# Stores of the latent queries' pairs of heads, written as one store of 64 rows for each head

## The chip, the cores and the metric

The kernel runs on one core of one Trainium2 chip. The metric is the device time of one execution in microseconds (us), as the median of several runs. A measurement of this kernel can tell about 0.2% (5.5 us) from no change. The core has TensorE (PE in the profile), VectorE (DVE), ScalarE (ACT), GpSimd (POOL) and SyncE (SP). All DMAs of this kernel are issued by SP, in one order, on one queue, and the bytes are moved by the core's 16 DMA engines.

## The reference, cut to what matters

Two layers run over 512 latent tokens and 256 context tokens. In each layer, one input projection feeds three attention branches. The change touches the first of them, multi-head latent attention (MLA), and of that only the queries: a normed latent of 384 features is projected to 8 heads of 96 features, 64 plain ones and 32 rotated ones.

```python
def mla_heads(qc, kvc, kr, q_norm, w_uq, kv_norm, w_ukv, rope):
    b, n = qc.shape[:2]
    q = (rms_norm(qc, q_norm) @ w_uq).reshape(b, n, MLA_HEADS, MLA_NOPE + MLA_ROPE)
    ...
    q_nope, q_rot = q[..., :MLA_NOPE], q[..., MLA_NOPE:]
    ...
    return (jnp.concatenate([q_nope, q_rot], axis=-1), jnp.concatenate([k_nope, k_rot], axis=-1), v)
```

## The kernel before, in words

All tensors are float32. Every matrix product is done as three products of rounded parts: a value x is split into a high part H, rounded by ACT, and a low part L = x - H, made by DVE. A weight item goes the same way: SP loads it into a tile `ws` (two buffers), ACT makes `wh` high and DVE makes `wh` low, and only then can PE use it. A `ws` buffer is loaded again when both parts of its last item are made.

The order of the work is written by a planner (`Plan`), which runs while the program is built. It keeps an estimated time for each engine and for the DMA queue (`dma_t`: 620 ns for each issue on the queue, then the bytes at 350 bytes per ns for all engines together), and it interleaves two streams of work. One stream is attention (scores into tiles `wd`, softmax, transposes by the helper at L913, products into `bk`); the other is the list `SEQ` of projections with their weights. What the planner writes is a fixed order for each engine.

The projections of the MLA queries stand near the head of each layer's list, as `cr p0 p1 Q3 p2 p3`, beside the attention of the windowed branch. `cr` makes the rotated features of all heads and stores them with four DMAs of 8 heads x 16 rows. Each `p` makes the plain features of a pair of heads: PE writes 128 rows (two heads of 64) and up to 768 tokens into `bk`, ACT and DVE make H and L in two slots (tiles `s`, from a pool of 46), and both are stored to the DRAM tensors `q_d`, of 8 heads x 96 rows x 768 tokens. The attention reads them back much later, head by head (the first of these loads is issued at 788.1 us). A slot is free for its next user when its store has landed; the function `chain` inside `uq_h` (L1368) tells the planner the estimated time of that. In layer 0 a stored row is 768 tokens (3072 bytes, 384 KB for a pair), in layer 1 it is 512 tokens (2048 bytes, 256 KB).

SP issues DMAs strictly in order. The DMAs signal their landing on eight semaphores in turn, so that a DMA also waits for the one issued eight before it.

Of the kernel before, what the change touches and what calls it, by code (L numbers as in the profile page):

```python
# [16 lines left out]
F32 = mybir.dt.float32  # L17
# [8 lines left out]
CT, LT, T = 256, 512, 768  # L26
# [209 lines left out]
def hybrid_kernel(tc, x_in, c_in, ctx_in, c_ctx, w_mod, b_mod, norm_g, w_in, q_norm, w_uq, kv_norm, w_ukv,  # L236
# [20 lines left out]
    def slot(dt=F32, cols=T):  # L257
        Slots.left -= 1
        assert Slots.left >= 0
        return sb.tile([128, cols], dt, name=nm("s"), tag="slot", bufs=NS)  # L260

    def free(n, when=None):
        def later():
            yield when
            Slots.left += n
        if when is None:
            Slots.left += n
        else:
            P.spawn(later(), 0)
# [77 lines left out]
    def dmas(ready, pairs):  # L347
        yield ready
        t = 0.0
        for o, i in pairs:  # L350
            t = max(t, dma(o, i))
        return t
# [21 lines left out]
    q_d = [[dr.tile([8, 96, T], F32, name=f"q{l}{s}") for s in range(2)] for l in range(2)]  # L374
# [4 lines left out]
    def wl_in(w, c0, k0=0, kn=8, n=128):  # L379
        def load(t):  # L380
            return [(t[:, 0:kn * n].rearrange("p (k c) -> p k c", k=kn),
                     w[k0 * 128:(k0 + kn) * 128, c0:c0 + n].rearrange("(k p) c -> p k c", p=128))]
        return load

    def item(load, parts=None, split=True, size=1024):

        done = When()
        return dict(load=load, parts=parts, split=split, size=size, ready=When(), done=done, staged=When() if split else done)
# [50 lines left out]
    def v3(it, k, n, off=0):  # L439
        return [it[s][:, off:off + k * n].rearrange("p (k c) -> p k c", k=k) for s in ("H", "L")]  # L440
# [21 lines left out]
    def fm(it, wv, X, kn, lat=True, ctx=True):  # L462

        r = {}
        if lat:
            r["l"] = {}
            yield from fm_part(it, wv, X, kn, CT, LT, bk.gate, r["l"])
        if ctx:
            r["c"] = {}
            yield from fm_part(it, wv, X, kn, 0, CT, bk.gate, r["c"])  # L470
        return r

    def split_to(t, src, H, L, scale=1.0, psum=True):

        t1 = yield from act(t, H, src, scale=scale, psum=psum)
        if scale == 1.0:
            t2 = yield from tt(t1, L, src, H.bitcast(F32), ALU.subtract)
        else:
            t2 = yield from stt(t1, L, src, scale, H.bitcast(F32), ALU.mult, ALU.subtract)
        return t2  # L480
# [717 lines left out]
    def entry(handler, its=(), need=0, keep=0, gate=0.0, ahead=False):  # L1198
        part[0].append((handler, list(its), need, keep, gate, ahead))
# [86 lines left out]
    def build_layer(o):  # L1286
        l = o.l
# [7 lines left out]
        def sec_q():  # L1295
# [18 lines left out]
            c0q = 0 if cx else CT  # L1314
# [44 lines left out]
            for pr in range(4):  # L1359
                pv = (lambda t: t[:, 0:384].rearrange("p (k h c) -> p k h c", k=3, h=2),  # L1360
                      lambda t: t[:, 0:576].rearrange("p (k h c) -> p k h c", k=3, h=2)[:, :, :, 0:64])
                n_it = item(wl_in(w_uq[l], pr * 192, kn=3, n=192), parts=[pv])

                def uq_h(it, pr=pr):
                    H, L = slot(F32R), slot(F32R)
                    r = yield from fm(it, v3(it, 3, 128), o.cq, 3, ctx=cx)

                    def chain():  # L1368
                        t = 0.0
                        for key, a, n in (("l", CT, LT), ("c", 0, CT)):  # L1370
                            if key in r:
                                t = yield from split_to(r[key]["t"], r[key]["ps"][:, 0:n], H[:, a:a + n], L[:, a:a + n])
                                r[key]["rel"].t = t
                        prs = []
                        for i, S_ in enumerate((H, L)):
                            prs.append((q_d[l][i][2 * pr:2 * pr + 2, 0:64, c0q:T], S_[:, c0q:T].bitcast(F32)))
                        t = yield from dmas(t, prs)
                        free(2, t)
                        yield o.qrt
                        for hh in range(2):  # L1380
                            o.qd[2 * pr + hh].t = max(t, o.qrt.t)
                    P.spawn(chain())
                    o.uses["cq"] -= 1
                    if not o.uses["cq"]:
                        free(6, P.now)
                entry(uq_h, [n_it], need=2)
# [537 lines left out]
```

## Time and profile before

| | |
|---|---|
| median of 3 runs | 2775.6 us (2774.97 to 2778.2) |
| the profiled execution, its own time | 2790.33 us |
| its span in the trace | 2788.6 us |
| PE busy | 2678.3 us, 96% of the span |
| DVE busy | 1656.1 us, 59% |
| ACT busy | 1382.4 us, 50% |
| mean DMA rate | 89 GB/s |
| pair stores in the program | 16 (4 pairs x H and L x 2 layers) |

PE is the engine with the most work, so its busy share is the first thing to read, then the stretches in which it is idle, and what ended them. In a table by windows, each engine has its busy time in the window with the number of its instructions in parentheses (in the order PE, PEld, DVE, ACT, POOL). The last three columns are the granted TensorE clock (1.00 is 2.4 GHz, 0.50 is 1.2 GHz), the mean busy share of the 16 DMA engines, and GB/s.

### The profile page before, as it was taken

Reading aid. Unit: us, or ns where it says so; the run is one execution under the profiler, and the core shown is the slowest. Engines: PE = TensorE matmul, PEld = TensorE weight load, DVE = VectorE, ACT = ScalarE, POOL = GpSimd, SP = SyncE. Lnnn points to the kernel's source line nnn. Section 1 sums busy time; section 2 is a strip of 40 time slices with the busy share of each in tenths; the row PEclk is TensorE's granted clock in tenths of the full one; section 3 lists DMA queues with packets and bytes.
Section 4 is the critical chain, followed back from the end, with each engine's and each line's share of the span. In section 5 each row is a group of like instructions: output and inputs, shape, how many; then the busy total and the mean of one; then the engine's idle time right before and its main releaser. Section 6 shows DMA issues by size and latency. Waiting matters only on the chain.

```text
span 2788.6 us, 42903 instructions
## 1 busy us (share of the span) xinstructions
PE 2678.3 (96%) x16711; PEld 2325.5 (83%) x16711; DVE 1656.1 (59%) x3350; ACT 1382.4 (50%) x2860; POOL 129.7 (5%) x198
## 2 busy tenths in 40 slices
PE   7998999999999999999999998899999999999998
PEld 4887898888888878878888987788888889888888
DVE  4676778666676652132423567698767677634435
ACT  4666777555556541121222356687645555523322
POOL 0000000111100000000000000000101100000000
PEclk8989999999999999999999999999999999999999
DMA  6123221111123353343322532322111123444433
GB/s 230 44 67 99 59 55 47 48 42 53 43 69 88 105 182 106 113 156 91 95 80 61 170 104 62 97 66 59 48 47 52 50 74 92 128 120 125 122 102 129
DMA packets 327867, 249.57 MB, mean 89 GB/s; under 512 B 24068, under 2 KB 287840, under 8 KB 327664
## 3 DMA queue, kind: packets, MB, share of 16 engines
q1 hardware_dynamic: 327664, 246.83, 30.2%
q8 instruction: 131, 2.15, 0.3%
q14 instruction: 72, 0.59, 0.1%
HBM read 211.37 MB, written 35.41 MB: 88 GB/s over the span
## 4 chain that ended last, share of the span: by engine, by line
PE 76%; DVE 8%; ACT 6%; DMA 5%; issue 3%; POOL 1%; SPq 1%; DVEq 0%; ACTq 0%; POOLq 0%
PE wd L444 36%; PE bk L444 34%; PE bk L913 4%; ACT s L309 3%; ACT pt L309 3%; DMA ws<-in_w_in_dram 2%; DVE pt L323 2%; DVE s L323 1%; DMA q<-s 1%; DVE wh L323 1%; DVE s L858 1%; PE bk L579 1%; DMA s<-in_w_mod_dram 1%; DVE s L330 1%; ACT wh L309 1%
## 5 line engine op out<-in xcount | busy, mean ns | idle before, releaser
L444 PE MATMUL wd<-s,wh 128*128 128x512 f32 (+1 forms) x4392 | 857.0, 356 | 7.0 <-ACT wh L309 3.8
L444 PEld LDWEIGHTS wd<-s,wh 128*128 128x128 f32 x4392 | 726.7, 190 | 145.8 <-ACT s L309 12.9
L444 PE MATMUL bk<-s,wh 128*128 128x512 f32 (+1 forms) x3666 | 778.6, 358 | 17.8 <-DVE s L323 6.8
L444 PEld LDWEIGHTS bk<-s,wh 128*128 128x128 f32 x3666 | 587.6, 191 | 107.3 <-DVE s L323 10.0
L323 DVE TENSOR_TENSOR wh<-ws,wh 128x1024 fp32r<-128x1024 f32 (+4 forms) x294 | 325.3, 1112 | 352.9 <-ACT wh L309 349.5
L309 ACT ACTIVATE wh<-ws 128x1024 fp32r<-128x1024 f32 (+4 forms) x294 | 282.8, 968 | 316.2 <-PE wd L444 148.7
L309 ACT ACTIVATE pt<-bk 128x512 fp32r<-128x512 f32 (+3 forms) x604 | 341.6, 584 | 171.6 <-PE bk L913 103.5
L444 PE MATMUL bk<-wh,s 128*128 128x256 f32 x2688 | 354.9, 287 | 3.8 <-DVE wh L323 2.0
L444 PEld LDWEIGHTS bk<-wh,s 128*128 128x128 f32 x2688 | 335.4, 194 | 9.5 <-issue 3.2
L323 DVE TENSOR_TENSOR pt<-bk,pt 128x512 fp32r<-128x512 f32 (+3 forms) x400 | 257.9, 664 | 87.9 <-ACT pt L309 77.1
L444 PE MATMUL bk<-pt,s 128*128 128x256 f32 x1888 | 282.3, 291 | 25.5 <-DVE pt L323 20.1
L444 PEld LDWEIGHTS bk<-pt,s 128*128 128x128 f32 x1888 | 256.3, 194 | 52.3 <-DVE pt L323 27.3
L444 PE MATMUL wd<-s,s 128*128 128x256 f32 (+5 forms) x1872 | 277.4, 334 | 12.2 <-DVE ti L858 6.6
L309 ACT ACTIVATE s<-wd,ti 128x768 f32<-128x768 f32 (+1 forms) x240 | 195.5, 818 | 140.8 <-DVE ti L825 78.6
L444 PEld LDWEIGHTS wd<-s,s 64*128 64x128 f32 (+2 forms) x1872 | 215.6, 191 | 43.0 <-ACT s L309 9.9
L913 PE MATMUL bk<-ident,s 128*128 128x128 f32 x1472 | 211.1, 278 | 15.8 <-DVE s L323 5.5
L913 PEld LDWEIGHTS bk<-ident,s 128*128 128x128 f32 x1472 | 172.1, 143 | 42.2 <-ACT s L309 7.6
L309 ACT ACTIVATE s<-s,ti 128x512 f32<-128x512 f32 (+3 forms) x249 | 174.4, 709 | 14.3 <-DVE ti L865 7.0
L309 ACT ACTIVATE s<-bk 128x256 fp32r<-128x256 f32 (+5 forms) x291 | 113.7, 424 | 92.6 <-PE bk L444 85.5
L330 DVE SCALAR_TENSOR_TENSOR s<-s,wd 128x768 f32<-128x768 f32 (+1 forms) x58 | 47.6, 820 | 180.7 <-PE wd L444 108.3
L309 ACT ACTIVATE s<-wd 128x768 f32<-128x768 f32 (+1 forms) x58 | 40.9, 705 | 219.3 <-PE wd L444 219.1
L825 DVE TENSOR_REDUCE ti<-wd 128x1 f32<-128x768 f32 (+1 forms) x160 | 128.8, 844 | 18.6 <-PE wd L444 18.3
(98 smaller groups left out, 1742.7 us busy)
## 6 DMA issues: line engine op xcount, KB each, us to landing
ws<-in_w_in_dram SPq DMA_DIRECT2D x180, 512.0 KB
ws<-in_w_branch_dram SPq DMA_DIRECT2D x48, 512.0 KB
ws<-in_w_mod_dram SPq DMA_DIRECT2D x32, 512.0 KB
ws<-in_w_out_dram SPq DMA_DIRECT2D x24, 512.0 KB
y<-yo SPq DMA_DIRECT2D x80, 128.0 KB
s<-y SPq DMA_DIRECT2D x24, 384.0 KB
s<-s SPq DMA_DIRECT2D x22, 384.0 KB
s<-in_w_mod_dram SPq DMA_DIRECT2D x32, 256.0 KB
```

What stands on the lines that cost most here:

```text
L309: lambda: nc.scalar.activation(out=out, in_=in_, func=func, scale=scale, **kw))
L323: t = yield from dve(ready, lambda: nc.vector.tensor_tensor(out=out, in0=a, in1=b, op=op), n)
L330: t = yield from dve(ready, lambda: nc.vector.scalar_tensor_tensor(out=out, in0=a, scalar=s, in1=b, op0=op0, op1=op1), fsz(out), ptr=ptr)
L444: nc.tensor.matmul(o, lhsT=l, rhs=r, start=first, stop=last)
L579: nc.tensor.matmul(pm[32 * g:32 * g + 32, :], lhsT=sil[:, kt], rhs=wv, start=kt < 4, stop=kt >= 4)
L825: t = yield from dve(t, lambda: nc.vector.tensor_reduce(out=nmx, in_=p[:, lo:hi], axis=AX.X, op=ALU.max, negate=True), n)
L858: t = yield from dve(t, lambda: nc.vector.tensor_tensor_reduce(out=pt_[:, 0:n], in0=p[:, lo:hi], in1=mk, scale=1.0, scalar=sk, op0=ALU.add ...
L913: nc.tensor.transpose(out=pp[:, j * 256 + ri2 * 128:j * 256 + ri2 * 128 + 128], in_=row["P"][:, c:c + 128], identity=ident)
```

## The change

The tuple of slices that `dmas` stores is built for each head of the pair instead of for the pair. Before, the DRAM side is a block of 2 heads x 64 rows x tokens, filled from the 128 rows of one slot. Now there are two stores of 64 rows x tokens each. The bytes, their rows and their places in DRAM are the same; the pair stores become 32 instead of 16.

```diff
                         for i, S_ in enumerate((H, L)):
-                            prs.append((q_d[l][i][2 * pr:2 * pr + 2, 0:64, c0q:T], S_[:, c0q:T].bitcast(F32)))
+                            for hh in range(2):
+                                prs.append((q_d[l][i][2 * pr + hh, 0:64, c0q:T], S_[hh * 64:hh * 64 + 64, c0q:T].bitcast(F32)))
```

On the SP queue of layer 1, where the first two pairs and the rotated features are stored, this stood before (`q` are the stores to `q_d`, `ws` weight loads, `y` stores of attention outputs from `yo`; the last numbers are the shape of what is written):

```order
L341 DMA y_99<-yo_17438 64x128 x2
L341 DMA q_104<-s_17514 2x64x512
L341 DMA q_105<-s_17515 2x64x512
L341 DMA q_104<-s_17447 8x16x512
L341 DMA q_104<-s_17449 8x16x512
L341 DMA q_105<-s_17448 8x16x512
L341 DMA q_105<-s_17450 8x16x512
L341 DMA q_104<-s_17559 2x64x512
L341 DMA q_105<-s_17560 2x64x512
L341 DMA ws_17648<-in_mla_w_uq_dram 128x3x192
L341 DMA ws_17684<-in_w_in_dram 128x8x128
```

The same place on the SP queue after the change:

```order
L341 DMA y_99<-yo_17446 64x128 x2
L341 DMA q_104<-s_17522 64x512 x2
L341 DMA q_105<-s_17523 64x512 x2
L341 DMA q_104<-s_17455 8x16x512
L341 DMA q_104<-s_17457 8x16x512
L341 DMA q_105<-s_17456 8x16x512
L341 DMA q_105<-s_17458 8x16x512
L341 DMA q_104<-s_17567 64x512 x2
L341 DMA q_105<-s_17568 64x512 x2
L341 DMA ws_17654<-in_mla_w_uq_dram 128x3x192
L341 DMA ws_17696<-in_w_in_dram 128x8x128
```

Nothing has moved against anything else here: each pair store has become two in its place, and the weight load behind them has four more DMAs ahead of it. At the other seven places of the queue it is the same.

The planner's estimates move with the number of DMAs, and in one place of the whole program another order came out of them. It is on PE, a few matmuls after the first pair stores of layer 1. Before, between two rows of scores (tiles `wd`), one round of transposes stood alone:

```order
L913 MATMUL bk_66<-ident,s_17474 128x128
L913 MATMUL bk_66<-ident,s_17486 128x128
L444 MATMUL wd_71<-s_16532,s_16906 128x384
L444 MATMUL wd_71<-s_16533,s_16906 128x384
L444 MATMUL wd_71<-s_16532,s_16906 128x256
L444 MATMUL wd_71<-s_16533,s_16906 128x256
L913 MATMUL bk_67<-ident,s_17474 128x128
L913 MATMUL bk_67<-ident,s_17486 128x128
L444 MATMUL wd_70<-s_16532,s_16907 128x384
L444 MATMUL wd_70<-s_16533,s_16907 128x384
```

After the change, the same place on PE:

```order
L913 MATMUL bk_66<-ident,s_17482 128x128
L913 MATMUL bk_66<-ident,s_17494 128x128
L913 MATMUL bk_67<-ident,s_17482 128x128
L913 MATMUL bk_67<-ident,s_17494 128x128
L444 MATMUL wd_71<-s_16540,s_16914 128x384
L444 MATMUL wd_71<-s_16541,s_16914 128x384
L444 MATMUL wd_71<-s_16540,s_16914 128x256
L444 MATMUL wd_71<-s_16541,s_16914 128x256
L444 MATMUL wd_70<-s_16540,s_16915 128x384
L444 MATMUL wd_70<-s_16541,s_16915 128x384
```

Two transposes moved ahead of four score matmuls. The orders of DVE, ACT and POOL are the same in both programs.

## Rows read from the trace of the kernel before

**Rows 1.** The page: busy time of the engines; the last chain by line.
```profile
PE 2678.3 (96%) x16711; PEld 2325.5 (83%) x16711; DVE 1656.1 (59%) x3350; ACT 1382.4 (50%) x2860; POOL 129.7 (5%) x198
PE wd L444 36%; PE bk L444 34%; PE bk L913 4%; ACT s L309 3%; ACT pt L309 3%; DMA ws<-in_w_in_dram 2%; DVE pt L323 2%; DVE s L323 1%; DMA q<-s 1%; DVE wh L323 1%; DVE s L858 1%; PE bk L579 1%; DMA s<-in_w_mod_dram 1%; DVE s L330 1%; ACT wh L309 1%
```

**Rows 2.** Chain that ended last, 200:262 and 1715:1800: start us, us, what.
```profile
214.72 18.07 DMA q<-s
235.28 18.41 DMA ws<-in_w_in_dram
...
1722.85 13.30 DMA q<-s
1738.00 14.81 DMA ws<-in_mla_w_uq_dram
1764.60 12.95 DMA ws<-in_w_in_dram
```

**Rows 3.** Timeline of PE: start us, us, what; in brackets idle before, releaser.
```profile
234.25 1.11 PE L913 MATMUL bk<-ident,s 128*128 128x128 f32 x4 [3.94 <-DVE s L323]
...
255.30 0.38 PE L444 MATMUL bk<-pt,s 128*128 128x256 f32 x1 [2.59 <-ACT pt L309]
256.68 1.86 PE L444 MATMUL bk<-pt,s 128*128 128x256 f32 x7 [0.99 <-DVE pt L323]
...
1737.22 1.22 PE L444 MATMUL wd<-s,s 128*128 128x256 f32 x4 [5.36 <-DVE ti L858]
...
1754.76 1.22 PE L444 MATMUL bk<-pt,s 128*128 128x256 f32 x4 [8.42 <-DVE pt L323]
...
1779.40 1.30 PE L913 MATMUL bk<-ident,s 128*128 128x128 f32 x9 [2.02 <-ACT s L309]
```

**Rows 4.** Table by windows: the four stretches at half the granted clock.
```profile
232.50:239.20 6.70, 4.95 (x14) 4.08 (x15) 3.68 (x10) 4.27 (x11) 0.00 (x0) 0.50 0.15 41
256.40:259.50 3.10, 2.82 (x12) 2.82 (x13) 0.82 (x2) 0.44 (x2) 0.00 (x0) 0.50 0.13 50
1734.50:1741.10 6.60, 3.88 (x11) 3.30 (x12) 4.50 (x18) 3.21 (x9) 0.00 (x0) 0.50 0.26 93
1751.50:1758.10 6.60, 3.34 (x9) 2.75 (x10) 3.82 (x6) 4.78 (x9) 0.00 (x0) 0.50 0.34 90
```

**Rows 5.** Table by windows: pair store, rotated store, 128-row store, 64-row store.
```profile
229.00:231.50 2.50, 1.31 (x6) 0.75 (x4) 0.21 (x2) 0.00 (x0) 0.00 (x0) 1.00 0.13 52
...
193.00:194.00 1.00, 0.97 (x7) 0.82 (x7) 0.91 (x4) 1.00 (x3) 0.00 (x0) 1.00 0.52 206
...
295.50:297.00 1.50, 1.50 (x11) 1.38 (x10) 1.50 (x4) 0.74 (x2) 0.00 (x0) 1.00 0.65 262
...
319.00:319.25 0.25, 0.25 (x5) 0.25 (x4) 0.25 (x1) 0.00 (x0) 0.00 (x0) 1.00 0.60 146
```

**Rows 6.** Timeline of SP: start us, us of issuing, what, count of issues.
```profile
294.84 0.34 SPq L341 DMA_DIRECT2D s<-s  x1
317.93 1.08 SPq L341 DMA_DIRECT2D y<-yo  x2
...
1722.20 15.71 SPq L341 DMA_DIRECT2D q<-s  x8
```

**Rows 7.** Waits, ACT 215:262, then ACT, DVE 1726:1782: total us, times, longest.
```profile
ACT s L309 <- DMA q<-s: 5.1, 1, 5.1
...
ACT wh L309 <- DMA ws<-in_mla_w_uq_dram: 10.2, 1, 10.2
...
DVE s L858 <- DMA q<-s: 6.1, 2, 5.2
```

**Rows 8.** Table by windows: the two stretches with the stores, and one behind.
```profile
220.00:262.00 42.00, 33.90 (x190) 29.48 (x189) 24.61 (x73) 22.67 (x54) 1.29 (x1) 0.88 0.29 89
1726.00:1781.00 55.00, 37.51 (x200) 31.92 (x199) 29.95 (x77) 28.81 (x61) 1.29 (x1) 0.88 0.34 100
262.00:300.00 38.00, 36.42 (x232) 32.02 (x231) 32.84 (x90) 29.93 (x70) 2.59 (x2) 1.00 0.32 93
```

## The prediction, made before the changed kernel ran

> **What bounds the kernel now.** The page comes first: PE is busy for 96% of the span, and the chain that ended last is mostly PE's own matmuls [rows 1]. So time can only be won where PE stands still, or where it runs at a lower clock. The changed stores are named in that chain, with 1% [rows 1]; hence the next view is the chain in order of time around them. It holds five DMA pieces: two are pair stores, of 18.07 and 13.30 us from issue to landing, and three are weight loads that were issued behind pair stores, of 18.41, 14.81 and 12.95 us [rows 2]. That is long for transfers of 256 to 512 KB, so the question is why.
>
> The table by windows answers. Where a pair store is alone in flight, the 16 DMA engines are busy for 0.13 of their time and move 52 GB/s [rows 5]. 0.13 of 16 is two engines, at about 26 GB/s each. A 128-row store of the same 384 KB (`s<-s`, issued at 294.84 [rows 6]) is over within one window of 1.5 us: 262 GB/s x 1.5 us = 393 kB [rows 5]. A pair store of 384 KB takes 393 kB / 52 GB/s = 7.6 us on its two engines, H and L together 15 us; in layer 1 it is 5.0 and 10 us. A weight load is spread over all engines, so its share on those two lands only behind the stores queued there, and it counts as landed when the last share is in.
>
> Three things then stop the other engines. An ACT or DVE instruction waits for a slot whose pair store has not landed: ACT 5.1 us in layer 0, DVE up to 5.2 us in layer 1 [rows 7]. ACT waits for a weight load: 10.2 us for the one issued at 1738.00 [rows 7]. And SP itself is held: it spends 15.71 us on eight stores, where two 64-row stores take it 1.08 us [rows 6].
>
> PE's own timeline shows what this costs. Its waits behind those pieces are 3.94 us (slot, layer 0), 2.59 + 0.99 us (weight load at 235.28, layer 0), 5.36 us (slot, layer 1), 8.42 us (weight load at 1738.00) and 2.02 us (weight load at 1764.60) [rows 3]: **23.3 us** in all. After the first four of these stalls, the granted clock is 0.50 for a while (1.2 instead of 2.4 GHz), and PE is busy at that clock for 4.95 + 2.82 + 3.88 + 3.34 = 15.0 us [rows 4]. At the full clock, this work takes half: another **7.5 us**. Together 30.8 us.
>
> **The change part by part.** *The form of the store.* The DRAM side loses its outer dimension of 2. What decides the number of engines must be read from the forms. The block of 2 x 64 rows ran on 2 engines; the rotated store, a block of 8 x 16 rows, ran at a share of 0.52, which is 8 engines; 64-row stores (`y<-yo`, issued at 317.93 [rows 6]) reach 0.60, over 9 engines at once even as a mean of a quarter us [rows 5]. So the outermost dimension sets it, and 64 rows should use all 16. Bounds for the two halves of a pair tile: at best the 1.5 us of the 128-row store of as many bytes, at worst the 7.6 us of before. I take 1.5 us, since its row has the same bytes and row length, and the 64-row form is seen on many engines.
>
> The Trainium skill states the rule outright ("DMA: Bandwidth & Descriptors", section "Why a DMA increments its semaphore by 16 and not by 1"): the engines used are the largest number up to 16 that divides the slowest non-unit dimension of both sides. It gives 2, 8 and 16 for the three forms, and the shares above agree for the first two.
>
> *The stalls.* With stores that land 2 to 3 us after their issue, both slot waits go: the stores were issued at 214.72 and 1722.85 [rows 2], and the waiting instructions stood ready only some 13 and 8 us later (18.07 - 5.1 and 13.30 - 5.2 [rows 2, 7]). The three weight loads go back to what a load takes alone, and nothing else is ahead of them, except in layer 1. There the four rotated stores keep their 8 engines: 4 x 262 kB / 206 GB/s [rows 5] = 5.1 us, from about 1724.4 (1722.20 and four issues) to 1729.5. The load behind them is issued at 1738.00 now, after SP's 15.71 us. With 12 stores at the 0.54 us that a 64-row store costs SP [rows 6], it would be issued at 1722.2 + 12 x 0.54 = 1728.7 at the earliest, some 1731 if SP waits for data, and land around 1734 (the 128-row store of 384 KB is over some 2 us after its issue [rows 5, 6]). ACT wanted it 10.2 us before 1752.84, at 1742.6; without the stall and the half clock ahead of it (5.36 + 1.9 us), it wants it at 1735.4. That is about 1 us of margin, so I set aside 2 us for this.
>
> *The added issues.* 16 more issues at 0.54 us are 8.7 us on SP in all, about 1.1 us at each of eight places. What is queued behind them is the next weight load and the stores of `yo`; who waits is ACT for `ws`. The cover is that SP's held-up time is longer than this at each place (15.71 us for eight issues, of which 4.3 are plain issue) and goes away. I cost it at 0; without that cover it is 8.7 us, and the third rival stands on it. Each pair also takes four of the eight landing semaphores instead of two; the DMA eight behind waits for stores that have landed by then.
>
> *The moved transposes.* Two transposes ahead of four score matmuls shift either by less than 1.2 us, and the engines' work is unchanged: 0, within 0.5 us either way.
>
> *What is late next.* Without the stalls, DVE and ACT lose their pauses too. In the two stretches PE is busy for 33.90 + 37.51 = 71.4 of 97 us [rows 8]; less the 7.5 us, 63.9 us of work are left. Behind them, at 262 to 300, PE is busy for 36.42 of 38 us, with DVE at 86% [rows 8]. At that share, the 63.9 us take 66.7 us, 30.3 us less than 97, and DVE's 54.6 us fill 82% of it: no more than in the stretch behind. So DVE does not become the bound, and both ways of counting agree. I take off 2 us for the rotated stores and 2 us for small waits of ACT and DVE in denser stretches: 30.8 - 4 = **27 us**.
>
> The sum stands against the profiled execution: 2790.3 - 27 = 2763 us. That execution is 14.7 us above the median of the runs; I carry the difference over as it is, so 2775.6 - 27 = **2748.6 us**.
>
> **The rivals.** *First: the rotated stores take the place of the pair stores in layer 1.* For it: they hold 8 engines for 5.1 us in the middle of the same queue, SP issues them between the pairs, and my margin there is 1 us. Against: they land by about 1730, and the long hold came behind the two-engine queue. If the 8.42 us wait with its half clock (1.7) stays whole, and the 5.36 us wait with its 1.9 stays by half, 30.8 - 10.1 - 3.6 - 2 = 15 us are won: 2760 us.
>
> *Second: the halves do not spread*, so that the change doesn't do what it says: the two stores of 64 rows share the old two engines, 7.6 us for both. Nothing changes then: 2776 us, within 0.2%. Against it stands the share of 0.60 for 64-row stores [rows 5].
>
> *Third, slower: the halves do not spread, and the added issues come on top.* SP's queue is what weight loads wait in, and at the places in [rows 2] ACT waits for loads. If the stores hold the engines as long as before, each added issue goes straight onto the next load: 16 x 0.54 = 8.7 us, 2784 us. It decides where the store time per pair stays above some 6 us, so that no gap is left on SP.
>
> The Trainium skill has a rule on this side (same page, section "Rules for kernel authors"): two transfers to disjoint halves of the partitions are not worth it, since both use all 16 engines anyway, and one transfer of 128 partitions is better. By that rule the result would be this rival's. The trace does not bear out its premise here, as the one transfer ran at a share of 0.13.
>
> **How the numbers follow.** The forecast, 2744 to 2756 us, gets 0.65; the first rival, up to 2765 us, 0.18; a win beyond 31 us, where places outside the listed stalls gain as well, 0.04; the second rival 0.09; the third 0.04. Less than 0.2% (5.5 us) cannot be told from no change. Faster by more than that: 0.65 + 0.18 + 0.04 = 0.87; same 0.09; slower 0.04. The range of 8 in 10 goes from 2742 us (33.6 us won) to 2763 us, which takes in the first rival's 2760; the price of the store between 1.5 and 7.6 us lies inside it down to a win of about 13 us.
>
> **What would show it.** In the profile of the changed kernel: around the pair stores the share of busy DMA engines is near 1 and not 0.13; no pair store in the chain; weight loads there under 5 us; SP's 12 stores in layer 1 take under 9 us; the waits of 3.94, 3.58, 5.36, 8.42 and 2.02 us are gone, and so are the stretches at clock 0.50 behind them. It is wrong if the share stays at 0.13, or if PE's waits stay under other names, on the rotated stores or on DVE and ACT.

## The result, and the profile after

| kernel | median of its runs | before beside it | ratio, 95% interval |
|---|---|---|---|
| changed kernel | 2752.2 us | 2776.9 us | 0.9896 [0.9881, 0.9912] |
| changed kernel, measured again | 2750.7 us | 2780.8 us | 0.9887 [0.9869, 0.9906] |

The change is faster by 1.0 to 1.1%: 24.7 us by the medians of the first comparison, 30.1 us by those of the second, where 27 us had been forecast. The ratios are not those of the medians beside them; their intervals stand for 24.4 to 33.0 us and 26.1 to 36.4 us. The profiled execution of the changed kernel has a span of 2745.0 us.

The page of the changed kernel (busy time of the engines, and the last chain by line) answers to [rows 1]:

```profile
PE 2657.7 (97%) x16711; PEld 2308.7 (84%) x16711; DVE 1655.3 (60%) x3350; ACT 1380.5 (50%) x2860; POOL 127.8 (5%) x198
PE wd L444 37%; PE bk L444 35%; PE bk L913 4%; ACT pt L309 3%; ACT s L309 3%; DVE pt L323 2%; DVE s L323 2%; PE bk L579 1%; DVE wh L323 1%; DVE s L858 1%; DVE s L330 1%; ACT wh L309 1%; DMA ws<-in_w_in_dram 1%; DVE ti L825 0%; POOL pt L325 0%
```

The pair stores have left this list of the chain, and DVE and ACT do the same work as before. Next, SP's timeline (start, us of issuing, what, count) at the third pair of layer 0 and at the first two pairs of layer 1, to be read against [rows 6]:

```profile
225.00 2.38 SPq L341 DMA_DIRECT2D q<-s  x4
...
1703.27 10.92 SPq L341 DMA_DIRECT2D q<-s  x12
```

Twelve stores take SP 10.92 us where eight took 15.71. The table by windows (columns as in the section on the profile) shows a stretch with pair stores in flight, then one with the rotated stores of layer 1, then the two stretches of [rows 8] as they are now, and the 38 us behind the first:

```profile
226.00:229.00 3.00, 3.00 (x17) 2.59 (x17) 3.00 (x10) 2.95 (x8) 0.00 (x0) 1.00 0.89 233
1709.00:1712.00 3.00, 2.54 (x18) 1.92 (x16) 3.00 (x9) 0.39 (x2) 0.00 (x0) 1.00 0.53 169
...
220.00:249.00 29.00, 28.54 (x182) 25.71 (x182) 23.15 (x69) 21.36 (x51) 1.29 (x1) 1.00 0.54 150
1709.00:1743.00 34.00, 32.18 (x187) 27.48 (x186) 28.74 (x77) 26.51 (x57) 1.29 (x1) 1.00 0.66 177
249.00:287.00 38.00, 36.42 (x233) 32.08 (x232) 32.93 (x93) 30.12 (x70) 2.59 (x2) 1.00 0.20 52
```

Around the pair stores the 16 DMA engines are busy for 0.89 of the time, at 233 GB/s, where it was 0.13 and 52 GB/s [rows 5]. The granted clock stays at 1.00. The 38 us behind the first stretch hold the same PE work as before, 36.42 us, only 13 us earlier.

How much each stretch gave can be read from the same matmuls in both timelines of PE. The changed kernel:

```profile
218.34 0.93 PE L444 MATMUL bk<-s,wh 128*128 128x512 f32 x3
250.22 1.32 PE L444 MATMUL bk<-s,wh 128*128 128x256 f32 x9
...
1694.91 4.92 PE L444 MATMUL bk<-s,wh 128*128 128x512 f32 x21
1720.39 0.74 PE L444 MATMUL bk<-pt,s 128*128 128x256 f32 x4 [1.03 <-DVE pt L323]
1750.53 2.31 PE L444 MATMUL bk<-s,wh 128*128 128x512 f32 x9
```

The same four groups in the kernel before:

```profile
219.19 0.94 PE L444 MATMUL bk<-s,wh 128*128 128x512 f32 x3
262.92 1.32 PE L444 MATMUL bk<-s,wh 128*128 128x256 f32 x9
...
1713.87 4.92 PE L444 MATMUL bk<-s,wh 128*128 128x512 f32 x21
1789.02 2.32 PE L444 MATMUL bk<-s,wh 128*128 128x512 f32 x9
```

In layer 0 the lead grows from 0.85 us (219.19 - 218.34) to 12.70 us: 11.85 us. In layer 1 it grows from 18.96 to 38.49 us: 19.53 us. Together the two stretches give **31.4 us**. The two profiled spans differ by 43.6 us; the other 12.2 us come from outside the two stretches. PE's 1.03 us wait at 1720.39 is the longest that is left in either stretch of this profile.

### The profile page after: what moved, and what is told of

Its sections match the earlier page's. It is cut to its first block, busy times and chain, and to the rows that moved or that the text cites. A ratio compares the mean times of both kernels' runs of the same rounds, so it can differ in the third digit from the quotient of the medians.

```text
span 2745.0 us, 42932 instructions
## 1 busy us (share of the span) xinstructions
PE 2657.7 (97%) x16711; PEld 2308.7 (84%) x16711; DVE 1655.3 (60%) x3350; ACT 1380.5 (50%) x2860; POOL 127.8 (5%) x198
## 4 chain that ended last, share of the span: by engine, by line
PE 78%; DVE 9%; ACT 7%; issue 3%; DMA 2%; POOL 1%; SPq 0%; DVEq 0%; ACTq 0%; POOLq 0%
PE wd L444 37%; PE bk L444 35%; PE bk L913 4%; ACT pt L309 3%; ACT s L309 3%; DVE pt L323 2%; DVE s L323 2%; PE bk L579 1%; DVE wh L323 1%; DVE s L858 1%; DVE s L330 1%; ACT wh L309 1%; DMA ws<-in_w_in_dram 1%; DVE ti L825 0%; POOL pt L325 0%
```

## The experiments

All ratios are against the kernel before, run beside it on the same chip. Where an experiment says that the order is that of before, the planner was told of one store per tile, so that PE, DVE and ACT keep exactly the order of the kernel before and SP keeps the place of each store.

**The kernel before, profiled once more.** No edit.

> The kernel before once more, for a second profile of it. The first profile was 14.7 us above the median of its runs. If the five waits of PE around the pair stores (23.3 us) belong to the kernel, they stand here too, within 2 us each, and the span is somewhere in 2773 to 2790 us. If they were a mishap of that one execution, most of them are absent.

Measured: 2785.8 us, a span of 2784.1 us. PE's timeline has the five waits again (the first in layer 0, the last three in layer 1):

```profile
234.75 1.12 PE L913 MATMUL bk<-ident,s 128*128 128x128 f32 x4 [4.54 <-DVE s L323]
255.75 0.39 PE L444 MATMUL bk<-pt,s 128*128 128x256 f32 x1 [2.67 <-ACT pt L309]
...
1737.31 1.22 PE L444 MATMUL wd<-s,s 128*128 128x256 f32 x4 [5.40 <-DVE ti L858]
1754.84 1.23 PE L444 MATMUL bk<-pt,s 128*128 128x256 f32 x4 [7.61 <-DVE pt L323]
1779.43 1.30 PE L913 MATMUL bk<-ident,s 128*128 128x128 f32 x9 [1.20 <-ACT s L309]
```

They are within 0.9 us of [rows 3]: the waits belong to the kernel. Against the second profile of the changed kernel (span 2751.4 us) the spans differ by 32.7 us. In this second pair of profiles PE starts the same four groups of matmuls at 219.11, 263.72, 1713.88 and 1789.05 us before, and at 213.28, 245.15, 1696.88 and 1752.63 us after. The lead grows by 12.74 us in layer 0 and by 19.42 us in layer 1, together 32.2 us, and 0.5 us is left outside the two stretches. So the 12.2 us outside them in the first pair are a difference between executions.

**As many stores, still on two engines.** Each pair store is cut by tokens instead of by heads.

```diff
-                            prs.append((q_d[l][i][2 * pr:2 * pr + 2, 0:64, c0q:T], S_[:, c0q:T].bitcast(F32)))
+                            cm = (c0q + T) // 2
+                            for a, b in ((c0q, cm), (cm, T)):
+                                prs.append((q_d[l][i][2 * pr:2 * pr + 2, 0:64, a:b], S_[:, a:b].bitcast(F32)))
```

> Each pair store is cut in two by tokens, so that both halves are still blocks of 2 heads x 64 rows: as many DMAs as in the changed kernel, of the same bytes, and PE's order is that of the changed kernel too. Theory (the two engines are the cause): two engines still, share 0.13 around the stores, time within 0.4% of before, 2768 to 2788 us. Rival (smaller stores that land apart, or the moved transposes, are the cause): about 2752 us.

Measured: 2786.3 us beside 2781.2, ratio 1.0022 [1.0010, 1.0033]. In its table by windows, and on PE:

```profile
222.00:224.00 2.00, 2.00 (x16) 1.87 (x15) 1.96 (x5) 1.93 (x4) 0.00 (x0) 1.00 0.13 51
```

```profile
232.67 1.12 PE L913 MATMUL bk<-ident,s 128*128 128x128 f32 x4 [5.37 <-DVE s L323]
...
1748.64 1.22 PE L444 MATMUL bk<-pt,s 128*128 128x256 f32 x4 [10.04 <-DVE pt L323]
```

The share is 0.13, and all the waits stand (the other three are 2.58, 4.95 and 1.47 us). Neither the number of stores nor the order with the moved transposes, which this kernel shares with the changed one, gives anything. The kernel is even some 0.2% slower than before.

**One store for each head, on two engines or on sixteen.** Both kernels cut each head's 64 rows in two, have 64 stores instead of 16, and the order of before. They differ in where the cut is: 62 and 2 rows, or 32 and 32.

```diff
-                            prs.append((q_d[l][i][2 * pr:2 * pr + 2, 0:64, c0q:T], S_[:, c0q:T].bitcast(F32)))
+                            for hh in range(2):
+                                for a, b in ((0, 62), (62, 64)):     # or ((0, 32), (32, 64))
+                                    prs.append((q_d[l][i][2 * pr + hh, a:b, c0q:T], S_[hh * 64 + a:hh * 64 + b, c0q:T].bitcast(F32)))
...     # the planner is told of one store for each tile
```

> One store for each head as in the changed kernel, but cut into 62 and 2 rows; the order on PE, DVE and ACT is that of the kernel before. Theory (the number of engines is the largest divisor of the rows up to 16, and it decides): 62 and 2 rows both run on 2 engines, share 0.13, time as before or up to 0.5% slower for 48 more issues, 2770 to 2792 us. Rival (the outer dimension of 2 heads costs, any plain block of rows is spread): about 2752 us.

> As the one with 62 and 2 rows, but cut into 32 and 32 rows: the same number of DMAs, the same order. Theory: 32 rows run on 16 engines, and the time is that of the changed kernel, 2746 to 2758 us, since the added issues on SP hide. Rival (added issues on SP cost): 32 more issues than the changed kernel at 0.54 us give up to 17 us more, about 2768 us.

Measured: 2786.2 us beside 2781.2 with 62 and 2 rows, ratio 1.0018 [1.0003, 1.0033]; 2754.2 us with 32 and 32 rows, ratio 0.9908 [0.9885, 0.9930]. In the tables by windows, first 62 and 2 rows, with its longest wait of ACT in 200 to 265 us, then 32 and 32 rows, with the one wait of PE over 1 us that is left there:

```profile
230.00:231.00 1.00, 1.00 (x9) 0.83 (x8) 0.05 (x1) 0.00 (x0) 0.00 (x0) 1.00 0.14 55
```

```profile
ACT wh L309 <- DMA ws<-in_w_in_dram: 13.4, 2, 9.1
```

```profile
227.00:230.00 3.00, 3.00 (x16) 2.44 (x15) 3.00 (x9) 2.98 (x9) 0.00 (x0) 1.00 0.91 212
```

```profile
1728.80 0.74 PE L444 MATMUL bk<-pt,s 128*128 128x256 f32 x4 [1.76 <-DVE pt L323]
```

This is the sharpest of the experiments. The bytes, the number of stores, the order and the plain shape of rows x tokens are the same. Only the number of rows differs, and with it the share of the engines, 0.14 or 0.91, and the whole gain. The Trainium skill's rule ("DMA: Bandwidth & Descriptors", section "Why a DMA increments its semaphore by 16 and not by 1": the largest divisor up to 16) says 2 engines for 62 rows and 16 for 32; both shares agree with it. What the 32 issues that this kernel has beyond the changed one cost, if anything, is inside its interval, which is some 6 us wide either way.

**The changed kernel again, and with the old order on PE.** The first has no edit. The second issues the changed kernel's stores but counts one for each tile in the plan:

```diff
-                        t = yield from dmas(t, prs)
+                        yield t
+                        t = 0.0
+                        for n, (out_, in_) in enumerate(prs):
+                            nc.sync.dma_start(out=out_, in_=in_)
+                            if n % 2:
+                                t = max(t, dma_t(2 * 4 * 64 * (T - c0q)))
```

> The changed kernel once more, in more rounds, for a narrower interval: 2746 to 2756 us; and a second profile of it, in which the pair stores again run on 16 engines and PE has none of the five waits.

> The changed kernel with the planner told of one store for each tile, so that the order on PE is that of the kernel before (the two transposes do not move). Theory (the order is worth nothing): the same as the changed kernel within 0.15%, 2747 to 2757 us. Rival (the moved transposes carry part of the gain): 2760 us or more.

Measured: 2750.7 us beside 2780.8, ratio 0.9887 [0.9869, 0.9906]; with the old order 2752.5 us, ratio 0.9901 [0.9887, 0.9916]. The intervals overlap: no effect of the moved transposes can be seen. The second profile of the changed kernel has a share of 0.94 around the pair stores (221 to 224 us) and none of the five waits; the longest in its shortened stretch of layer 1 is 0.33 us.

**Layer 0 alone.**

```diff
+                            if l == 1:
+                                prs.append((q_d[l][i][2 * pr:2 * pr + 2, 0:64, c0q:T], S_[:, c0q:T].bitcast(F32)))
+                                continue
                             for hh in range(2):
                                 prs.append((q_d[l][i][2 * pr + hh, 0:64, c0q:T], S_[hh * 64:hh * 64 + 64, c0q:T].bitcast(F32)))
```

> One store for each head in layer 0 alone, layer 1 as before; order as before. Theory (the gain is the two groups of stalls, added up): layer 0 gives 3.94 + 3.58 us of waits and 3.7 us of half clock, 11 us, so 11 us less than the kernel before, and its PE waits of 5.36, 8.42 and 2.02 us in layer 1 stand as they were. Rival (a stall removed early is given back at the next one): within 4 us of the kernel before.

Measured: 2770.0 us beside 2780.8, 10.8 us less, ratio 0.9964 [0.9950, 0.9978]. PE in layer 1:

```profile
1716.86 1.22 PE L444 MATMUL wd<-s,s 128*128 128x256 f32 x4 [5.45 <-DVE ti L858]
1734.39 1.22 PE L444 MATMUL bk<-pt,s 128*128 128x256 f32 x4 [7.66 <-DVE pt L323]
1758.95 1.31 PE L913 MATMUL bk<-ident,s 128*128 128x128 f32 x9 [1.21 <-ACT s L309]
```

The interval stands for 6 to 14 us. That holds the 11 us of the layer's stalls and leaves out the rival's less than 4 us, and the waits of layer 1 stand as in the second profile of before: the stall removed early is not given back at the next one.

**One store of 128 rows on sixteen engines.** The plain rows get a DRAM tensor in which a pair is 128 rows; the later loads of a head are two instead of one.

```diff
...     # the DRAM tensors
-                            prs.append((q_d[l][i][2 * pr:2 * pr + 2, 0:64, c0q:T], S_[:, c0q:T].bitcast(F32)))
+                            prs.append((qn_d[l][i][128 * pr:128 * pr + 128, c0q:T], S_[:, c0q:T].bitcast(F32)))
...
-                    t = max(t, dma(Q[s][0:96, c0:T].bitcast(F32), q_d[l][i][h, :, c0:T]))
+                    nc.sync.dma_start(Q[s][0:64, c0:T].bitcast(F32), qn_d[l][i][64 * h:64 * h + 64, c0:T])
+                    nc.sync.dma_start(Q[s][64:96, c0:T].bitcast(F32), q_d[l][i][h, :, c0:T])
+                    t = max(t, dma_t(4 * 96 * (T - c0)))
```

> The plain rows of all heads go to a DRAM tensor of their own with 512 rows, so that a pair tile is one store of 128 rows: 16 stores as in the kernel before. The later loads of a head become two (64 and 32 rows), 32 DMAs more there; order of the engines as before. Theory (16 engines decide, not the cutting into heads): as the changed kernel, 2746 to 2757 us. Rival (the cutting by heads is the cause): about 2780 us.

Measured: 2748.0 us beside 2780.8, ratio 0.9888 [0.9872, 0.9904]. Sixteen stores, as before, and the gain of the changed kernel: it is the engines and not the cutting. In the table by windows, at the third pair of layer 0, the pair of the changed kernel's window of 226 to 229 us:

```profile
221.50:223.50 2.00, 2.00 (x14) 1.74 (x13) 2.00 (x8) 1.95 (x6) 0.00 (x0) 1.00 0.84 339
```

At about the same share of busy engines the 128-row stores move 339 GB/s and the 64-row stores 233. So the share tells how many engines are at work, and not how fast they are. The kernel's time does not show the difference.

**Half of the two-engine bytes.** The high part is stored head by head, the low part as a pair; order of before.

```diff
+                            if i == 1:
+                                prs.append((q_d[l][i][2 * pr:2 * pr + 2, 0:64, c0q:T], S_[:, c0q:T].bitcast(F32)))
+                                continue
...     # the planner is told of one store for each tile
```

> Only the high parts are stored head by head; the low part of each pair is still one block of 2 x 64 rows, so that the two engines hold 7.6 us (layer 1: 5.0 us) of stores for each pair instead of 15 us (10 us); order as before. Theory (a stall arises only where a store or a load lands after it is wanted): in the kernel before, the waits were 5.1, 4.7, 5.2, 10.2 and 3.3 us, and landings come 5 to 10 us earlier, so nearly all of the gain is there, 2750 to 2760 us. Rival (time lost in proportion to the two-engine bytes): half of the gain, about 2765 us.

Measured: 2760.9 us beside 2782.2, ratio 0.9920 [0.9903, 0.9937]. That is 21.3 us less (17.5 to 27.0 us by the interval), just outside the theory's range and more than the rival's half of the gain. In layer 0 PE is busy for 60.58 of the 62 us from 200 to 262, so nothing is left to win there; in layer 1 two waits remain (PE's timeline, then the chain in order of time):

```profile
200.00:262.00 62.00, 60.58 (x394) 54.20 (x392) 51.47 (x144) 47.69 (x111) 2.60 (x2) 1.00 0.43 121
```

```profile
1714.25 0.74 PE L444 MATMUL wd<-s,s 128*128 128x256 f32 x4 [2.21 <-DVE ti L858]
1729.31 1.22 PE L444 MATMUL bk<-pt,s 128*128 128x256 f32 x4 [6.12 <-DVE pt L323]
```

```profile
1704.65 8.52 DMA q<-s
1715.55 11.81 DMA ws<-in_mla_w_uq_dram
```

My arithmetic for layer 1 counted only the pair stores. The four rotated stores put shares on the same two engines (4 x 262 kB / 8 = 131 kB on each, as much as one pair store), and the weight load stands behind all of them. That they are the same engines shows in the kernel before, where a pair store is in flight from 1722.85 for 13.30 us [rows 2] together with the rotated stores, at a share of 0.50, which is 8 of 16 engines and not 10:

```profile
1730.00:1734.00 4.00, 0.74 (x4) 0.54 (x4) 0.89 (x2) 0.27 (x1) 0.00 (x0) 1.00 0.50 147
```

So layer 0, where half of the bytes gave the whole gain, bears out the theory against the rival. For layer 1 its sum left out a part of the queue; with that part it fits, but this was worked out after the run.

**The same stores, issued by ACT.**

```diff
-                        t = yield from dmas(t, prs)
+                        yield t
+                        t = 0.0
+                        for n, (out_, in_) in enumerate(prs):
+                            nc.scalar.dma_start(out=out_, in_=in_)
...     # the planner is told of one store for each tile
```

> The stores of before, 2 x 64 rows on two engines, but issued by ACT on its own DMA queue instead of SP's; order of DVE and PE as before. If the weight loads are late because they stand behind the stores in one queue, the load waits go (2.59 + 0.99 + 8.42 + 2.02 us and their half clock) and the slot waits stay, less what ACT pays for issuing: 2760 to 2772 us. If the two engines themselves are what is short, whichever queue feeds them, the time stays within 0.3% of before; and if ACT is held at its issues as SP was, it is slower than before.

Measured: 2805.7 us beside 2782.2, ratio 1.0087 [1.0067, 1.0107]. The timelines of ACT and of PE in layer 0:

```profile
190.20 0.50 ACTq L1380 DMA_DIRECT2D q<-s  x1
199.42 13.16 ACTq L1380 DMA_DIRECT2D q<-s  x2
```

```profile
213.46 0.48 PE L913 MATMUL bk<-ident,s 128*128 128x128 f32 x1 [15.18 <-ACT s L309]
260.65 1.12 PE L913 MATMUL bk<-ident,s 128*128 128x128 f32 x4 [9.89 <-ACT s L309]
```

The third expectation came true: the second pair holds ACT for 13.16 us at two issues, and PE stands for 15.18 us behind it. The issuing engine paid for the two-engine stores here, ACT as SP before it. Whether the weight loads were late because of the common queue or because of the two engines themselves, this run does not settle, since ACT was late for another reason.

**The rotated stores on sixteen engines too.** As the kernel with 128-row stores, and the rotated rows go to DRAM tensors of 128 rows; a head's later loads are three.

```diff
...     # the DRAM tensors, and the plain rows as above
-                    prs = [(q_d[l][i][:, 64 + 16 * j:80 + 16 * j, c0q:T], R[j][i][:, c0q:T].bitcast(F32)) for i in range(2) for j in range(2)]
+                    prs = [(qr_d[l][i][j][:, c0q:T], R[j][i][:, c0q:T].bitcast(F32)) for i in range(2) for j in range(2)]
...     # the three loads of a head
```

> Plain rows as one store of 128 rows, and the rotated rows too, in DRAM tensors of 128 rows (16 engines instead of 8); the later loads of a head become three (64, 16 and 16 rows); order as before. Theory: no wait of PE stands on the rotated stores any more, as the changed kernel has no such wait left either; so the same as the changed kernel within 0.2%, 2744 to 2756 us. Rival (the rotated stores' 5 us on 8 engines still cost): 2740 us or less.

Measured: 2748.9 us beside 2782.2, ratio 0.9876 [0.9856, 0.9896]. The table by windows during the rotated stores of layer 0:

```profile
191.00:194.00 3.00, 1.76 (x13) 1.32 (x12) 3.00 (x12) 2.51 (x8) 0.00 (x0) 1.00 1.03 408
```

The stores run twice as fast as at 0.52 and 206 GB/s [rows 5], while PE is busy for 1.76 of the 3 us and DVE for all of them. The interval overlaps that of the changed kernel: no further gain is shown.

## Why the prediction was right, point by point

**The form of the store: right.** Read from three forms in the trace, it said that the outermost dimension sets the number of engines, 16 for 64 rows. The share around the pair stores is 0.89, and the two kernels with 62 + 2 and 32 + 32 rows show that the number of rows decides, as their largest divisor up to 16 would have it. A pair's 786 kB at the 233 GB/s of that window are 3.4 us, 1.7 us a tile against the 1.5 us taken.

**The stalls: right.** All five waits and the half-clock stretches behind four of them are gone. The sum of 30.8 us meets 31.4 and 32.2 us read from the two stretches in two pairs of profiles: 11.4 us against 11.85 and 12.74 in layer 0, 19.4 against 19.53 and 19.42 in layer 1. With layer 0 alone changed, the runs give 10.8 us.

**The two deductions: not seen in the stretches, 4 us.** For the rotated stores I had set 2 us aside; they became a 1.03 us wait in the first profile, and no such wait in the second. They do hold the queue (share 0.53 at 1709 to 1712 us), and my times for it were too short. SP takes 10.92 us for the twelve stores instead of the 9 us I gave it as a bound. The load behind them lands 15.2 us after the first store was issued (1714.28 + 4.16 - 1703.27), where I had 11.8 (1734 - 1722.2). So ACT waits for it, where I had seen a margin of 1 us (chain, then waits of ACT from 1703 to 1730 us):

```profile
1714.28 4.16 DMA ws<-in_mla_w_uq_dram
```

```profile
ACT wh L309 <- DMA ws<-in_mla_w_uq_dram: 0.8, 1, 0.8
```

The 2 us for denser DVE and ACT work did not come. PE is busy for 98% and 95% of the two shortened stretches (28.54 of 29 us, 32.18 of 34 us), against 96% of the 38 us behind the first; in layer 1 that is some 0.4 us. So the forecast of 27 us was 4 us below the sum of its own terms, and the stretches show the sum. The runs cannot tell the two apart: the intervals of the result hold 27 us as well as 31.

**The added issues at 0: right, with its condition.** With 16 engines even 48 added issues leave the gain whole within the interval (0.9908 [0.9885, 0.9930]). Where the stores stay on two engines, the kernels with 16 and with 48 more issues are both about 0.2% slower (1.0022 and 1.0018). That is the third rival's direction, but at 5 us and not the 8.7 us it was priced at. Three times as many issues did not cost more, so the price of 0.54 us for each does not describe it; where the 5 us come from, no run shows.

**The Trainium skill's rule against the change** ("DMA: Bandwidth & Descriptors", section "Rules for kernel authors": two transfers to disjoint partition halves are not worth it) holds where both run on all 16 engines. The measured 0.9888 of the kernel with one 128-row store agrees with it in the kernel's time: one whole transfer is as good as two halves, as long as the whole is spread.

**The profiled execution's excess.** The prediction carried its 14.7 us over as a constant. The changed kernel's profile shows no such excess (2746.8 us against runs of 2751.9 to 2753.2). It did no harm, because the stalls were summed as differences. The two profiled spans alone would have said 43.6 us.

## What to carry to other kernels

When a store or load is slow, look at the share of busy DMA engines while it is alone in flight, and count engines before bytes: a block whose outermost dimension is 2 ran on 2 of 16. Here the price was paid by the loads queued behind the stores, by the buffers that they freed late and by the engine that issued them. So add up everything that stands on those engines between the store and the load that is wanted.

## What the runs showed that I had not expected

The engine that issued stores onto the two busy engines was held for longer than one such store takes by itself (7.6 us in layer 0, 5.0 us in layer 1): ACT for 13.16 us at two issues in layer 0, SP for 15.71 us at eight in layer 1. And a head's 64 rows cut into 62 and 2 instead of 32 and 32 took back the whole gain of 1%, at the same bytes and as many stores.
